# Gate and up products with the activations stationary, two PSUM banks in turn, and a short warm-up

## The chip, the core and the metric

The kernel runs on one core of a Trainium2 chip. The metric is the device time of one execution in microseconds (us). Everything is float32 in and out; matrix products are made from a high part and a low part of each operand (below).

## The reference

Two layers of a transformer on 256 tokens of width 2048. Each layer is: half a SwiGLU feed-forward block (FFN), a mixer, half an FFN. Layer 0 has a gated delta-rule and pooling mixer (GDN), layer 1 a latent attention mixer (MLA). Only the FFN and the output projections of the mixers matter here.

```python
def swiglu(h, w_gate, w_up, w_down):
    return (jax.nn.silu(h @ w_gate) * (h @ w_up)) @ w_down

for layer in range(DEPTH):                    # DEPTH = 2
    x = x + 0.5 * swiglu(rms_norm(x, ffn1_norm[layer]), ...)   # gate, up: 2048 x 4096, down: 4096 x 2048
    h = rms_norm(x, mix_norm[layer])
    x = x + delta_pool_mixer(h, ...)  if layer % 2 == 0 else  x + mla_mixer(h, ...)
    x = x + 0.5 * swiglu(rms_norm(x, ffn2_norm[layer]), ...)
```

So there are four FFNs.

## The kernel before

**Split products.** Each float32 operand is split into a high part (a cast to the rounded type fp32r) and a low part (the rest). A product is high times high, plus low weight times high activation, plus high weight times low activation. Weights come from memory in tiles `raw` of 128 x 2048 (1 MB, three buffers, SyncE's queue). `piece` (L167, L168) makes of each half of such a tile a `whi` on ScalarE (ACT) and a `wlo` on VectorE (DVE), 128 x 1024, four buffers each. The normalized activations lie in 16 tiles `xg[k]` of 128 features x (high 256 tokens, low 256 tokens), made by `feed_part` (L155, L156).

**Gate and up, before.** The hidden width of 4096 goes in 32 blocks f of 128. For each f, `gemm` runs over the 16 k and `mm3` issues two products: the stationary operand is a 128 x 128 block of `whi`, and the moving operand is the whole of `xg[k]`, 512 columns (high and low tokens side by side in one PSUM bank); then a block of `wlo` is stationary and the high half, 256 columns, is moving. All products of one f go to one bank. The result is features x tokens, the layout that the down product needs. `scaled` adds the two halves (L436, L437), multiplies by the norm factor `R` (L438; `end_norm` spreads it over the partitions by a product on TensorE, L371), then come Silu (L131), gate times up (L459) and the split into the tiles `g` (L152, L153).

**Down and mixer outputs.** In `project` the activations are stationary (128 x 128: one half t of the tokens) and the weights move, 512 columns at a time. For each of 4 column blocks j and each k (32 for an FFN, 16 for a mixer) six products go out: three in a row to the bank of t = 0, three to the bank of t = 1. Then L398 adds the result to x.

**Order of work.** The program is written out by hand and a scheduler orders each engine's queue by it, with a model of the times. `Chains` holds generators (`spawn`, `poll`) whose steps are woken by a clock that the issued products move; `yield n * LAG` asks for a distance of n x 1500 ns of such clock. `feed_norm` uses this: four transposes on TensorE (L361) are put into a running product at such a distance after the values they need.

**Start.** `constants` calls `warm_up`: zeros are multiplied while the first loads are under way. Eight products of plain float32 (L281) are followed by rows of products of several forms (L288), among them one row of eight fp32r products of 512 columns into one bank and one row of eight in which two banks take turns, all with start and stop set. The first FFN then begins with `opening`, which loads the activations in four parts and the first two blocks f of gate and up.

PSUM has eight banks of 128 x 512 float32; in an FFN six serve products (`mm`) in rotation and two the transposes (`aux`).

Of the kernel before, what the change touches and what calls it, by code (L numbers as in the profile page):

```python
# [18 lines left out]
P = 128  # L19
S = 256  # L20
D = 2048
KT = 16
DFF = 4096
NF = 32
# [15 lines left out]
LAG = 1500.0  # L40
# [3 lines left out]
SILU = "silu_and_others"  # L44
# [53 lines left out]
class Builder:  # L98
# [89 lines left out]
    def gemm(self, ps, stream, acts, wide=True):  # L188

        K = len(acts)  # L190
        for k0 in range(0, K, 8):
            self.gemm_piece(ps, next(stream), acts, k0, wide)
# [76 lines left out]

    def warm_up(self):  # L270

        nc = self.nc
        z = self.tmp([P, S], "res")
        nc.vector.memset(z, 0.0)
        zr = self.wp.tile([P, 2048], F32R, tag="raw", bufs=3, name=self.nm("zr"))
        nc.vector.memset(zr.bitcast(F32), 0.0)
        zb = z.bitcast(BF16)
        self.banks(7, 1)
        ps = self.psum("aux")
        for n in range(8):  # L280
            nc.tensor.matmul(ps[:, 0:S], z[:, 0:P], z, start=n == 0, stop=n == 7)  # L281
        a, b = self.psum("mm"), self.psum("mm")
        w = zr[:, 1024:1152]

        def row(rhs, count, outs=(a,), lhsT=w):
            size = int(np.prod(rhs.shape[1:]))
            for n in range(count):
                nc.tensor.matmul(outs[n % len(outs)][:, 0:size], lhsT, rhs, start=True, stop=True)  # L288

        row(zr[:, 0:512], 8)  # L290
        row(zr[:, 0:512], 8, (a, b))
        row(zb, 6, lhsT=zb[:, 0:P])
        row(zr[:, 0:256], 8)
        row(zr[:, 0:384], 6)
        row(zr.rearrange("p (a c) -> p a c", a=2)[:, :, 0:256], 6)
        row(zr[:, 0:1024].rearrange("p (c a) -> p c a", a=2)[:, :, 0], 6)
        row(zr[:, 4:516], 6)
        row(zr[:, 16:528], 6)
        row(zr[:, None, 0:256].to_broadcast([P, 2, 256]), 6)
        row(z, 4, lhsT=z[:, 0:P])  # L300

    def load_xf(self, c):

# [64 lines left out]
    def end_norm(self, after):  # L368
# [3 lines left out]
        self.behind(m, after)  # L372
        R = self.tp.tile([P, S], F32, tag="R", bufs=1, name=self.nm("R"))
        self.nc.scalar.copy(R, ps[:, :S])
        return R

    def project(self, slabs, acts, half, after):

        K = len(acts)
        st = self.weights(*[slabs[j] for j in range(4)])  # L380
        blk = [slice(0, P), slice(P, 2 * P)]
        for j in range(4):
            ps = [self.psum("mm") for _ in range(2)]
            for k in range(K):
                if k % 2 == 0:
                    piece = next(st)
                hi, lo = (w[:, 512 * (k % 2) : 512 * (k % 2) + 512] for w in piece)
                self.ch.wait(lambda: acts[k] is not None)
                a = acts[k]
                for t in range(2):  # L390
                    self.mm(ps[t], a[:, 0, blk[t]], hi, start=k == 0, stop=False)
                    self.mm(ps[t], a[:, 0, blk[t]], lo, start=False, stop=False)
                    self.last_mm = self.mm(ps[t], a[:, 1, blk[t]], hi, start=False, stop=k == K - 1)
                self.ch.poll()
            for t in range(2):
                x = self.x[j][:, t, :]
                if half:
                    self.nc.vector.scalar_tensor_tensor(x, ps[t], 0.5, x, op0=ALU.mult, op1=ALU.add)  # L398
                else:
                    self.nc.vector.tensor_tensor(x, ps[t], x, op=ALU.add)  # L400
            after(j)


    def ffn(self, wg, wu, wd, after, start=False):
        nc, tc = self.nc, self.tc
        with tc.tile_pool(name=self.nm("gp"), bufs=1) as gp:
            self.banks(6, 2)
            xg = self.xg

            def opening():  # L410

                ps = [self.psum("mm") for _ in range(4)]
                for c in range(4):
                    raw = self.raw_tile()
                    k4 = slice(512 * c, 512 * c + 512)
                    self.load_xf(c)
                    for w, src in enumerate((wg, wu)):
                        dst = raw[:, 1024 * w : 1024 * w + 1024].rearrange("p (f k) -> p f k", f=2)
                        nc.sync.dma_start(dst, src[0:2, :, k4].rearrange("f p k -> p f k"))
                    for w in range(2):  # L420
                        hi, lo = self.piece(raw, 1024 * w)
                        for n in range(8):
                            k = 4 * c + n % 4
                            n128 = slice(n * P, n * P + P)
                            self.last_mm = self.mm3(ps[2 * (n // 4) + w], hi[:, n128], lo[:, n128], xg[k], k == 0, k == KT - 1, True)
                self.load_rest()
                return ps

            def ws():
                for f in range(2 if start else 0, NF):  # L430
                    yield from self.weights(wg[f], wu[f])

            def scaled(ps):

                t, u = (gp.tile([P, S], F32, tag=n, bufs=3, name=self.nm(n)) for n in ("t", "u"))
                nc.scalar.copy(u, ps[:, S : 2 * S])  # L436
                nc.vector.tensor_tensor(t, ps[:, 0:S], u, op=ALU.add)  # L437
                nc.vector.tensor_tensor(t, t, R, op=ALU.mult)  # L438
                return t

            st = ws()
            g = []
            early = opening() if start else []
            for f in range(NF):
                if early:
                    pg, pu = early.pop(0), early.pop(0)
                else:
                    pg, pu = self.psum("mm"), self.psum("mm")
                    self.gemm(pg, st, xg)
                    if f == 0:  # L450
                        self.gemm(pu, st, xg)
                if f == 0:
                    R = self.end_norm(self.last_mm)
                tg = scaled(pg)
                self.table(SILU, tg, tg, AF.Silu)
                if f > (1 if start else 0):
                    self.gemm(pu, st, xg)
                tu = scaled(pu)
                nc.vector.tensor_tensor(tu, tu, tg, op=ALU.mult)  # L459
                gt = gp.tile([P, 2, S], F32R, name=self.nm("g"))  # L460
                self.split_hi_lo(gt, tu)
                g.append(gt)
            self.project(wd, g, True, after)

    def store(self, j):
        for t in range(2):
# [3 lines left out]
def gdn(b, after):  # L470
# [7 lines left out]
    with tc.tile_pool(name="gd", bufs=1) as gp:  # L478
# [18 lines left out]
        for t in range(2):  # L497
# [321 lines left out]
def mla(b, after):  # L819
# [8 lines left out]
    with tc.tile_pool(name="ml", bufs=1) as gp:  # L828
# [183 lines left out]
        for p in range(MH // 2):  # L1012
# [57 lines left out]
def slabs(w):  # L1070

    K, N = w.shape
    return w.reshape(K // P, P, N // P, P).transpose(2, 1, 0, 3).reshape(N // P, P, K)


def wide_slabs(w):

    K = w.shape[0]
    return w.reshape(K // P, P, 4, 512).transpose(2, 1, 0, 3).reshape(4, P, 4 * K)


def columns(v, n):

    return v.reshape(n, P).T
# [20 lines left out]
def prepare(a):  # L1105
    n = {}
# [4 lines left out]
    g = [columns(a[k][l], KT) for l in range(2) for k in ("ffn1_norm", "mix_norm", "ffn2_norm")]  # L1111
    n["gains"] = np.stack(g, 1)
    for f in ("1", "2"):
        for s, k in (("g", "gate"), ("u", "up"), ("d", "down")):
            lay = wide_slabs if s == "d" else slabs
            n[f"w{f}{s}"] = np.stack([lay(a[f"ffn{f}_w_{k}"][l]) for l in range(2)])
    w = a["hyb_w_in"][0]
    u = slabs(np.concatenate([w[:, :4096], w[:, 4112:]], 1))
    n["wqk"] = np.stack([u[8 * c + h] for h in range(GH) for c in range(2)])
# [12 lines left out]
    w = a["hyb_w_out"][0]  # L1132
    n["wgo"] = wide_slabs(np.concatenate([w[:1024]] + [w[1024 + P * c : 1152 + P * c] for c in POOL_ORDER], 0))
    w = a["mla_w_in"][0]
# [38 lines left out]
```

## Time and profile before

| | |
|---|---|
| median of 2 runs | 2904.0 us (2903.99 to 2904.01) |
| profiled execution | 2904.99 us, of which the span of the trace is 2903.2 us |
| TensorE, products | busy 2895.9 us (100%), 16272 products |
| VectorE / ScalarE / GpSimd | busy 1776.9 us (61%) / 1462.9 us (50%) / 57.5 us (2%) |
| memory | 509.84 MB read, 176 GB/s over the span |

In the rows PE is TensorE (PEld its weight loads), DVE VectorE, ACT ScalarE. A product's duration in the rows includes a modelled tail that overlaps the next product; the distance from one start to the next is what TensorE's time is made of.

### The profile page before, as it was taken

Reading aid. Unit: us, or ns where it says so; the run is one execution under the profiler, and the core shown is the slowest. Engines: PE = TensorE matmul, PEld = TensorE weight load, DVE = VectorE, ACT = ScalarE, POOL = GpSimd, SP = SyncE. Lnnn points to the kernel's source line nnn. Section 1 sums busy time; section 2 is a strip of 40 time slices with the busy share of each in tenths; the row PEclk is TensorE's granted clock in tenths of the full one; section 3 lists DMA queues with packets and bytes.
Section 4 is the critical chain, followed back from the end, with each engine's and each line's share of the span. In section 5 each row is a group of like instructions: output and inputs, shape, how many; then the busy total and the mean of one; then the engine's idle time right before and its main releaser. Section 6 shows DMA issues by size and latency. Waiting matters only on the chain.

```text
span 2903.2 us, 39987 instructions
## 1 busy us (share of the span) xinstructions
PE 2895.9 (100%) x16272; PEld 2492.8 (86%) x16272; DVE 1776.9 (61%) x2532; ACT 1462.9 (50%) x2222; POOL 57.5 (2%) x97
## 2 busy tenths in 40 slices
PE   9999999999999999999999999999999999999999
PEld 8888888899998888888888888888898788888887
DVE  5666655576785666665546666645677566666544
ACT  5444444466374544444445444544577554444433
POOL 0000000000000000000000000000022000000000
PEclk9999999999999999999999999999999999999999
DMA  6555555544235555555555555555533445555554
GB/s 235 189 187 181 185 189 187 181 149 173 102 142 181 181 185 186 188 189 189 182 183 187 187 182 185 186 189 188 179 135 113 145 174 189 189 182 186 187 202 143
DMA packets 77256, 514.65 MB, mean 177 GB/s; under 512 B 10768, under 2 KB 11536, under 8 KB 16272
## 3 DMA queue, kind: packets, MB, share of 16 engines
q1 hardware_dynamic: 75344, 508.90, 49.4%
q8 instruction: 127, 2.08, 0.3%
q0 software_dynamic: 576, 2.10, 0.2%
q10 hardware_dynamic: 1152, 1.10, 0.1%
q14 instruction: 57, 0.47, 0.1%
HBM read 509.84 MB, written 2.10 MB: 176 GB/s over the span
## 4 chain that ended last, share of the span: by engine, by line
PE 98%; issue 1%; ACT 0%; DVE 0%; POOL 0%; DMA 0%; ACTq 0%; POOLq 0%; DVEq 0%
PE mm L186 92%; PE aux L186 4%; PE mm L288 1%; PE aux L361 1%; PE aux L281 0%; PE aux L681 0%; PE aux L997 0%; ACT sq L336 0%; POOL osq L221 0%; DMA cb<-in_wab 0%; PE aux L371 0%; ACT L126 0%; ACT whi L167 0%; ACT xg L155 0%; DVE x L398 0%
## 5 line engine op out<-in xcount | busy, mean ns | idle before, releaser
L186 PE MATMUL mm<-xg,whi 128*128 128x512 f32 (+1 forms) x5664 | 1720.6, 368 | 0.6 <-ACT xg L155 0.3
L168 DVE TENSOR_TENSOR wlo<-raw,whi 128x1024 fp32r<-128x1024 f32 x960 | 1175.2, 1225 | 747.1 <-ACT whi L167 737.5
L167 ACT CAST whi<-raw 128x1024 fp32r<-128x1024 f32 x960 | 1007.0, 1049 | 761.3 <-PE mm L186 736.5
L186 PE MATMUL mm<-xg,wlo 128*128 128x256 f32 x4880 | 1329.6, 281 | 0.0
L186 PEld LDWEIGHTS mm<-xg,whi 128*128 128x128 f32 x5664 | 997.7, 189 | 168.6 <-DVE xg L156 1.5
L186 PEld LDWEIGHTS mm<-xg,wlo 128*128 128x128 f32 x4880 | 923.2, 189 | 25.7
L186 PE MATMUL mm<-whi,g 128*128 128x512 f32 x2048 | 648.5, 396 | 0.0
L186 PEld LDWEIGHTS mm<-whi,g 128*128 128x128 f32 x2048 | 384.0, 187 | 92.9
L186 PE MATMUL mm<-wlo,g 128*128 128x512 f32 x1024 | 404.5, 395 | 0.0
L436 ACT COPY u<-mm 128x256 f32<-128x256 f32 x256 | 95.1, 372 | 463.4 <-PE mm L186 463.4
L437 DVE TENSOR_TENSOR t<-mm,u 128x256 f32<-128x256 f32 x256 | 108.6, 425 | 246.8 <-ACT u L436 246.7
L186 PEld LDWEIGHTS mm<-wlo,g 128*128 128x128 f32 x1024 | 192.0, 188 | 46.0
L438 DVE TENSOR_TENSOR t<-t,R 128x256 f32<-128x256 f32 x256 | 108.5, 425 | 8.4
L186 PE MATMUL mm<-whi,o 128*128 128x512 f32 x256 | 84.2, 399 | 0.0
L152 ACT CAST g<-t 128x256 fp32r<-128x256 f32 x128 | 52.1, 407 | 56.9 <-DVE t L459 56.9
L221 POOL TENSOR_TENSOR sq<-sqf,sq 128x256 fp32r<-128x256 f32 x49 | 45.4, 932 | 1337.2 <-ACT sq L220 1324.1
L186 PEld LDWEIGHTS mm<-whi,o 128*128 128x128 f32 x256 | 47.9, 187 | 11.1 <-DVE o L153 0.2
L459 DVE TENSOR_TENSOR t<-t,t 128x256 f32<-128x256 f32 x128 | 54.5, 426 | 4.8 <-ACT t L131 0.2
L155 ACT ACTIVATE xg<-aux,gains 128x256 fp32r<-128x256 f32 x80 | 37.1, 471 | 38.9 <-DVE xg L156 27.5
L131 ACT ACTIVATE t<-t 128x256 f32<-128x256 f32 x128 | 53.5, 418 | 5.8 <-DVE t L438 5.4
L153 DVE TENSOR_TENSOR g<-t,g 128x256 fp32r<-128x256 f32 x128 | 53.5, 418 | 0.0
L186 PE MATMUL mm<-wlo,o 128*128 128x512 f32 x128 | 50.5, 395 | 0.0
(267 smaller groups left out, 1560.6 us busy)
## 6 DMA issues: line engine op xcount, KB each, us to landing
raw<-in_w1d SPq DMA_DIRECT2D x64, 1024.0 KB, 4.8
raw<-in_w2g SPq DMA_DIRECT2D x64, 1024.0 KB, 4.8
raw<-in_w2u SPq DMA_DIRECT2D x64, 1024.0 KB, 4.8
raw<-in_w2d SPq DMA_DIRECT2D x64, 1024.0 KB, 4.8
raw<-in_w1g SPq DMA_DIRECT2D x62, 1024.0 KB, 4.8
raw<-in_w1u SPq DMA_DIRECT2D x62, 1024.0 KB, 4.8
raw<-in_wqk SPq DMA_DIRECT2D x16, 1024.0 KB, 4.8
raw<-in_wgo SPq DMA_DIRECT2D x16, 1024.0 KB, 4.8
```

The costliest lines, as they stand in the source:

```text
L131: a = nc.scalar.activation(out, in_, func, **kw)
L152: nc.scalar.copy(dst[:, 0, :], src)
L153: nc.vector.tensor_tensor(dst[:, 1, :], src, dst[:, 0, :].bitcast(F32), op=ALU.subtract)
L155: nc.scalar.activation(dst[:, 0, :], src, AF.Copy, scale=scale)
L167: self.nc.scalar.copy(hi, raw[:, h : h + 1024])
L168: self.nc.vector.tensor_tensor(lo, raw[:, h : h + 1024], hi.bitcast(F32), op=ALU.subtract)
L186: return self.nc.tensor.matmul(out, lhsT, rhs, start=start, stop=stop)
L221: nc.gpsimd.tensor_tensor(dst[:, 1, :], sq, dst[:, 0, :].bitcast(F32), op=ALU.subtract)
L436: nc.scalar.copy(u, ps[:, S : 2 * S])
L437: nc.vector.tensor_tensor(t, ps[:, 0:S], u, op=ALU.add)
L438: nc.vector.tensor_tensor(t, t, R, op=ALU.mult)
L459: nc.vector.tensor_tensor(tu, tu, tg, op=ALU.mult)
```

## The change

Gate and up are computed as the down product is: `columns` takes 512 hidden columns at a time (8 blocks instead of 32), the activations are stationary, the weights move. `rows` issues the six products of a k with the two banks (token halves t) in turn: high-high t0, t1; low weights t0, t1; low activations t0, t1. `project` uses the same functions, so the down products and both mixers' output projections take turns too. The result is now tokens x features: `gated` applies Silu with the norm factor `r2` as a scale per partition, `hidden` multiplies gate and up, transposes the 128 x 128 blocks back on TensorE (eight per block of 512) and splits them into `g`. `end_norm` is no longer called by the FFN. `opening` loads whole 1 MB tiles of the first 512 columns of gate and up. The weights of gate and up are laid out on the host as those of down are. The warm-up keeps its eight plain float32 products alone.

```diff
     def warm_up(self):
-        z = self.tmp([P, S], "res")
-        zr = self.wp.tile([P, 2048], F32R, tag="raw", bufs=3, name=self.nm("zr"))
...
+        z = self.tmp([P, S], "res", 1)
+        self.nc.vector.memset(z, 0.0)
         self.banks(7, 1)
         ps = self.psum("aux")
         for n in range(8):
+            self.nc.tensor.matmul(ps[:, 0:S], z[:, 0:P], z, start=n == 0, stop=n == 7)
-        row(zr[:, 0:512], 8)
-        row(zr[:, 0:512], 8, (a, b))
...
+    def rows(self, ps, hi, lo, act, first, last):
+        blk = [slice(0, P), slice(P, 2 * P)]
+        for part, w in ((0, hi), (0, lo), (1, hi)):
+            end = last and part == 1
+            for t in range(2):
+                self.last_mm = self.mm(ps[t], act[:, part, blk[t]], w, start=first and w is hi and part == 0, stop=end)
+
+    def columns(self, stream, acts):
+        K = len(acts)
+        ps = [self.psum("mm") for _ in range(2)]
+        for k in range(K):
+            if k % 2 == 0:
+                piece = next(stream)
+            hi, lo = (w[:, 512 * (k % 2) : 512 * (k % 2) + 512] for w in piece)
+            self.ch.wait(lambda: acts[k] is not None)
+            self.rows(ps, hi, lo, acts[k], k == 0, k == K - 1)
+            self.ch.poll()
+        return ps
+
     def project(self, slabs, acts, half, after):
         for j in range(4):
-                for t in range(2):
-                    self.mm(ps[t], a[:, 0, blk[t]], hi, start=k == 0, stop=False)
-                    self.mm(ps[t], a[:, 0, blk[t]], lo, start=False, stop=False)
-                    self.last_mm = self.mm(ps[t], a[:, 1, blk[t]], hi, start=False, stop=k == K - 1)
+            ps = self.columns(st, acts)
...
             def opening():
+                ps = [[self.psum("mm") for _ in range(2)] for _ in range(2)]
                 for c in range(4):
                     self.load_xf(c)
+                    raws = [self.raw_tile() for _ in range(2)]
+                    for raw, src in zip(raws, (wg, wu)):
+                        nc.sync.dma_start(raw, src[0][:, 2048 * c : 2048 * c + 2048])
+                    for h in range(2):
+                        for w in range(2):
+                            hi, lo = self.piece(raws[w], 1024 * h)
+                            for n in range(2):
+                                k = 4 * c + 2 * h + n
+                                c512 = slice(512 * n, 512 * n + 512)
+                                self.rows(ps[w], hi[:, c512], lo[:, c512], xg[k], k == 0, k == KT - 1)
...
+            def gated(ps):
+                sg = gp.tile([P, 2, 512], F32, tag="sg", bufs=2, name=self.nm("sg"))
+                for t in range(2):
+                    self.table(SILU, sg[:, t, :], ps[t], AF.Silu, scale=self.r2[:, t : t + 1])
+                return sg
+
+            def hidden(f, ps, sg):
+                for t in range(2):
+                    nc.vector.scalar_tensor_tensor(sg[:, t, :], ps[t], self.r2[:, t : t + 1], sg[:, t, :], op0=ALU.mult, op1=ALU.mult)
+                yield 1.5 * LAG
+                for h in range(2):
+                    pt = self.psum("aux")
+                    for n in range(2):
+                        for t in range(2):
+                            c = (2 * h + n) * P
+                            nc.tensor.transpose(pt[:, (2 * n + t) * P : (2 * n + t + 1) * P], sg[:, t, c : c + P], self.ident)
+                            self.ch.clock += P / 2.4
+                    gt = gp.tile([P, 2, 2, S], F32R, name=self.nm("g"))
+                    flat = lambda part: gt[:, part].rearrange("p n s -> p (n s)")
+                    nc.scalar.copy(flat(0), pt)
+                    nc.vector.tensor_tensor(flat(1), pt, flat(0).bitcast(F32), op=ALU.subtract)
+                    for n in range(2):
+                        g[4 * f + 2 * h + n] = gt[:, :, n, :]
+                    yield 0.5 * LAG
...
-            for f in range(NF):
+            for f in range(NC):
+                if f == 0 and start:
+                    pg, pu = opening()
+                    sg = gated(pg)
                 else:
+                    pg = self.columns(st, xg)
+                    sg = gated(pg)
+                    pu = self.columns(st, xg)
+                self.ch.spawn(hidden(f, pu, sg))
+                self.ch.poll()
+            self.project(wd, LateList(lambda k: g[k], NF), True, after)
```

## Rows read from the trace of the kernel before

**Rows 1.** The page: busy time by engine, and the granted clock in 40 slices.

```profile
PE 2895.9 (100%) x16272; PEld 2492.8 (86%) x16272; DVE 1776.9 (61%) x2532; ACT 1462.9 (50%) x2222; POOL 57.5 (2%) x97
...
PEclk9999999999999999999999999999999999999999
```

**Rows 2.** The page: the chain that ended last, by line.

```profile
PE mm L186 92%; PE aux L186 4%; PE mm L288 1%; PE aux L361 1%; PE aux L281 0%; PE aux L681 0%; PE aux L997 0%; ACT sq L336 0%; POOL osq L221 0%; DMA cb<-in_wab 0%; PE aux L371 0%; ACT L126 0%; ACT whi L167 0%; ACT xg L155 0%; DVE x L398 0%
```

**Rows 3.** Timeline of TensorE, last FFN: start us, duration us, instruction.

```profile
2369.14 0.59 PE L371 MATMUL aux<-dg,ca 128*128 128x256 f32 x2
2369.39 0.58 PE L186 MATMUL mm<-xg,whi 128*128 128x512 f32 x1
...
2719.97 0.39 PE L186 MATMUL mm<-whi,g 128*128 128x512 f32 x1
...
2898.23 0.63 PE L186 MATMUL mm<-whi,g 128*128 128x512 f32 x2
2898.69 0.40 PE L186 MATMUL mm<-wlo,g 128*128 128x512 f32 x1
2898.93 0.39 PE L186 MATMUL mm<-whi,g 128*128 128x512 f32 x1
```

**Rows 4.** Groups by form, 2370 to 2719 us: count, busy us, mean ns of one.

```profile
L186 PE MATMUL mm<-xg,whi 128*128 128x512 f32 x989 | 344.6, 399 | 0.0
L186 PE MATMUL mm<-xg,wlo 128*128 128x256 f32 x989 | 267.9, 281 | 0.0
```

**Rows 5.** Groups by form, 2721 to 2898 us.

```profile
L186 PE MATMUL mm<-whi,g 128*128 128x512 f32 x507 | 159.5, 395 | 0.0
...
L398 DVE SCALAR_TENSOR_TENSOR x<-mm,x 128x512 f32<-128x512 f32 x6 | 3.8, 683 | 0.0
```

**Rows 6.** Groups by form, 8.2 to 9.5 us: warm-up, one bank.

```profile
L288 PE MATMUL mm<-zr 128*128 128x512 f32 x7 | 1.8, 394 | 0.0
```

**Rows 7.** Groups by form, 9.95 to 11.2 us: warm-up, two banks in turn.

```profile
L288 PE MATMUL mm<-zr 128*128 128x512 f32 x7 | 1.7, 389 | 0.0
```

**Rows 8.** Groups by form, 20.25 to 21.35 us: warm-up, one bank, another offset.

```profile
L288 PE MATMUL mm<-zr 128*128 128x512 f32 x7 | 1.8, 392 | 0.0
```

**Rows 9.** Groups by form, 54.1 to 58.3 us: gate and up, first FFN.

```profile
L186 PE MATMUL mm<-xg,whi 128*128 128x512 f32 x12 | 4.2, 391 | 0.0
L186 PE MATMUL mm<-xg,wlo 128*128 128x256 f32 x14 | 3.8, 280 | 0.0
```

**Rows 10.** Timeline of TensorE around four transposes of feed_norm.

```profile
435.19 0.39 PE L186 MATMUL mm<-whi,g 128*128 128x512 f32 x1
435.41 0.60 PE L361 MATMUL aux<-ca,x 128*128 128x128 f32 x4
435.77 0.48 PE L186 MATMUL mm<-whi,g 128*128 128x512 f32 x1
436.09 0.39 PE L186 MATMUL mm<-wlo,g 128*128 128x512 f32 x1
```

**Rows 11.** Timeline of TensorE at the start.

```profile
1.22 6.63 PE L281 MATMUL aux<-res 128*128 128x256 f32 x16 [1.22 <-DVE res L274]
7.50 4.03 PE L288 MATMUL mm<-zr 128*128 128x512 f32 x16
...
24.45 0.91 PE L186 MATMUL mm<-xg,whi 128*128 128x512 f32 x2
```

**Rows 12.** Timeline of ACT at the start.

```profile
6.49 1.03 ACT L167 CAST whi<-raw 128x1024 fp32r<-128x1024 f32 x1
8.83 1.05 ACT L167 CAST whi<-raw 128x1024 fp32r<-128x1024 f32 x1 [1.31 <-DMA raw<-in_w1u]
...
11.78 1.03 ACT L167 CAST whi<-raw 128x1024 fp32r<-128x1024 f32 x1
```

**Rows 13.** Groups by form, 1 to 6 us: the first warm-up products.

```profile
L281 PE MATMUL aux<-res 128*128 128x256 f32 x11 | 5.1, 649 | 1.2 <-DVE res L274 1.2
```

**Rows 14.** Groups by form, 23 to 24 us: the last warm-up products.

```profile
L288 PE MATMUL mm<-res 128*128 128x256 f32 x6 | 1.5, 379 | 0.0
```

**Rows 15.** The page: splitting the weights on DVE.

```profile
L168 DVE TENSOR_TENSOR wlo<-raw,whi 128x1024 fp32r<-128x1024 f32 x960 | 1175.2, 1225 | 747.1 <-ACT whi L167 737.5
```

More of the change, by code (lines that the diff above doesn't have):

```diff
@@ L270, in warm_up @@
     def warm_up(self):
-        nc = self.nc
-        z = self.tmp([P, S], "res")
-        nc.vector.memset(z, 0.0)
-        zr = self.wp.tile([P, 2048], F32R, tag="raw", bufs=3, name=self.nm("zr"))
-        nc.vector.memset(zr.bitcast(F32), 0.0)
-        zb = z.bitcast(BF16)
+        z = self.tmp([P, S], "res", 1)
+        self.nc.vector.memset(z, 0.0)
         self.banks(7, 1)
@@ L280, in warm_up @@
         for n in range(8):
[L281 to L288, printed above, removed]
-        row(zr[:, 0:512], 8)
-        row(zr[:, 0:512], 8, (a, b))
[L292 to L300, printed above, removed]
+            self.nc.tensor.matmul(ps[:, 0:S], z[:, 0:P], z, start=n == 0, stop=n == 7)
     def load_xf(self, c):
@@ L375, in end_norm @@
         return R
+    def rows(self, ps, hi, lo, act, first, last):
[15 more added lines that the diff above has]
+        return ps
     def project(self, slabs, acts, half, after):
-        K = len(acts)
         st = self.weights(*[slabs[j] for j in range(4)])
-        blk = [slice(0, P), slice(P, 2 * P)]
         for j in range(4):
[L383 to L389, printed above, removed]
-                for t in range(2):
-                    self.mm(ps[t], a[:, 0, blk[t]], hi, start=k == 0, stop=False)
-                    self.mm(ps[t], a[:, 0, blk[t]], lo, start=False, stop=False)
-                    self.last_mm = self.mm(ps[t], a[:, 1, blk[t]], hi, start=False, stop=k == K - 1)
-                self.ch.poll()
+            ps = self.columns(st, acts)
             for t in range(2):
@@ L405, in ffn @@
         nc, tc = self.nc, self.tc
+        NC = DFF // 512
         with tc.tile_pool(name=self.nm("gp"), bufs=1) as gp:
@@ L408, in ffn @@
             xg = self.xg
+            g = [None] * NF
             def opening():
-                ps = [self.psum("mm") for _ in range(4)]
+                ps = [[self.psum("mm") for _ in range(2)] for _ in range(2)]
                 for c in range(4):
-                    raw = self.raw_tile()
-                    k4 = slice(512 * c, 512 * c + 512)
                     self.load_xf(c)
[L417 to L425, printed above, removed]
+                    raws = [self.raw_tile() for _ in range(2)]
[8 more added lines that the diff above has]
+                                self.rows(ps[w], hi[:, c512], lo[:, c512], xg[k], k == 0, k == KT - 1)
                 self.load_rest()
@@ L429, in ws @@
             def ws():
-                for f in range(2 if start else 0, NF):
+                for f in range(1 if start else 0, NC):
                     yield from self.weights(wg[f], wu[f])
[L433 to L439, printed above, removed]
@@ L441, in ffn @@
-            st = ws()
-            g = []
-            early = opening() if start else []
-            for f in range(NF):
-                if early:
-                    pg, pu = early.pop(0), early.pop(0)
-                else:
[L448 to L462, printed above, removed]
@@ L463, in ffn @@
-            self.project(wd, g, True, after)
+            def gated(ps):
[21 more added lines that the diff above has]
+                    yield 0.5 * LAG
@@ L1076, in wide_slabs @@
 def wide_slabs(w):
-    K = w.shape[0]
-    return w.reshape(K // P, P, 4, 512).transpose(2, 1, 0, 3).reshape(4, P, 4 * K)
+    K, N = w.shape
+    return w.reshape(K // P, P, N // 512, 512).transpose(2, 1, 0, 3).reshape(N // 512, P, 4 * K)
 def columns(v, n):
@@ L1114, in prepare @@
         for s, k in (("g", "gate"), ("u", "up"), ("d", "down")):
-            lay = wide_slabs if s == "d" else slabs
-            n[f"w{f}{s}"] = np.stack([lay(a[f"ffn{f}_w_{k}"][l]) for l in range(2)])
+            n[f"w{f}{s}"] = np.stack([wide_slabs(a[f"ffn{f}_w_{k}"][l]) for l in range(2)])
     w = a["hyb_w_in"][0]
```

## The prediction

> **What bounds the kernel now.** I read the page's busy times first: TensorE is busy for the whole span, VectorE for 61% and ScalarE for 50%, and the granted clock stands at full speed in every slice [rows 1]. The chain that ended last says the same from the other side: 92% of it is the line that issues all products [rows 2]. So only what changes TensorE's own time can count: the number of products, the distance from the start of one to the start of the next, and stretches in which it does something useless (the warm-up). Work taken from VectorE and ScalarE is worth nothing here, and it stays hidden as long as TensorE is not made to wait.
>
> The columns that gate and up stream do not change: 768 per k and block of 128 before (512 + 256), six times 512 per k and block of 512 after, which is again 768 per 128. What changes is how they are cut into products, so the distance between starts is the number to find. The timeline of the last FFN gives it. From 2369.39 to 2719.97 us there are 31 blocks x 2 x 16 = 992 pairs, 353.4 ns a pair [rows 3, 4]. From there to the last product at 2898.93 there are 767 steps of the down product, 233.3 ns each [rows 3]. A mean duration of 395 ns in the groups thus goes with a distance of 233 [rows 5]: the tail of 162 ns overlaps the next product, and I use that difference to turn other durations into distances.
>
> **The change part by part.**
>
> *Gate and up.* 4 FFNs x 32 x 2 x 16 = 4096 pairs cost 4096 x 0.3534 = 1447.5 us. They become 4 x 8 x 2 x 16 x 6 = 6144 products of 512 columns of the form that the down product has. At its 233.3 ns they cost 1433.4 us: 14.1 us less, from the cut alone.
>
> *Taking turns.* Does it shorten the distance? The warm-up holds the nearest rows. Seven products into one bank average 394 ns, the seven after them, with two banks in turn and nothing else changed, 389 [rows 6, 7]; a later row into one bank has 392 [rows 8]. The gain is 3 to 5 ns a product. These are products of zeros with one stationary block and without accumulation, so I also look for the effect in the body, where `project` changes bank after every third product. Across the change two products take 2898.69 - 2898.23 = 0.46 us, and the next, without a change, 2898.93 - 2898.69 = 0.24 [rows 3]: no gain at a single change. And the same one-bank pairs that average 399 and 281 ns in the last FFN average 391 and 280 for some microseconds of the first [rows 4, 9], so the distance can settle at several values with no change of bank at all. The bounds are therefore 0 and the full step down to the alternating row's own distance, 389 - 162 = 227 ns; I take the middle of the warm-up's gain, 4 ns, since only that row alternates at every product. The distance is then 229.3 ns: gate and up 6144 x 0.2293 = 1408.8 us, 38.7 less than before, and the down and output products, 4 x 4 x 32 x 6 + 2 x 4 x 16 x 6 = 3840, gain 3840 x 0.004 = 15.4 us.
>
> *Transposes.* Eight per block of 512, 4 x 8 x 8 = 256, in 64 groups of four, all on TensorE's path. Around such a group of `feed_norm` two products and four transposes take 436.09 - 435.19 = 0.90 us; less two products of 0.233 that is 0.433 us a group [rows 10]. 64 x 0.433 = 27.7 us are added. The groups carry 0.60 us for four, which is mostly tail. The Trainium skill (TensorE: Matmul & The Clock Gate, Part 4: PE-mode transpose) gives about 275 ns for a transpose in a kernel's context; as an estimate from that page 256 of them would cost 70 us and leave no gain. The row decides against it here: 0.11 us from start to start.
>
> *Waits that come with them.* The transposes need gate times up, which VectorE forms out of PSUM: two operations like L398's, 683 ns each [rows 5], behind at most one weight split of 1225 ns in flight [rows 15], 2.6 us after the last up product. `hidden` yields 1.5 x 1500 ns of product clock in between; that clock counts 213 ns for a product that really takes 229, so about 2.4 us of real products are queued ahead. The wait is 0 to 0.2 us a block, 0 to 6 us in all; I take 0, because TensorE's timeline shows none before the transposes that `feed_norm` places in the same way [rows 10]. Behind a late transpose the whole product stream is queued. The rest of the tail, ScalarE's copy and VectorE's subtraction, has 28 more steps of k before `project` reads the last `g`. ScalarE's Silu now waits for gate's last product with weight splits behind it, as its copy of the same result did before; four `whi` buffers, some 11 us of products, cover 1.3 us of Silu. SyncE's loads keep their size of 1 MB and their rate.
>
> *`end_norm`.* Two instructions and the product behind them start 0.25 us apart and stretch it from 0.40 to 0.58: 0.43 us [rows 3], four times, 1.7 us less.
>
> *Warm-up.* The first real product now starts at 24.45 us, because the rows of products run till then [rows 11]. The weights were there long before: the first 0.5 MB tile's half was being split at 6.49 us, the second at 8.83 [rows 12]. Now the first tile is 1 MB, so it lands when both of these had, about 8.8; its split takes 1.05 us, and the first product can start at 9.9. That is 14.5 us earlier. The up tile follows 1 MB later; by the next split's start, 11.78 after 8.83 [rows 12], it is ready at 12.8 against 12.65 when gate's first twelve products are through, 0.2 us of waiting. After that each quarter keeps TensorE for 11 us and loads 2.5 MB, at the start's pace 7 us: no further wait. There is a hole from 7.9 to 9.9 us, after the eight products that remain. The first products ran at the lower clock level (649 ns against 379 for the same form later, 1.2 against 2.4 GHz) from 1.22 us nearly to the start of the first row at 7.50 [rows 11, 13, 14], which cost about 2.8 us. If the hole brings that back it costs as much again; I take half, 1.3. The start saves 13.0 us, between 11 and 14.5.
>
> **Sum.** -38.7 - 15.4 + 27.7 - 1.7 - 13.0 = -41.1 us on the profiled execution, whose 2904.99 us lie 1.0 above the median of the runs. From the median 2904.0: 2863 us, 1.4% faster. Own range of this case, with 3 and 5 ns and the bounds of start and waits: 2848 to 2877.
>
> **The rivals.**
>
> 1. Taking turns pays nothing: the steps of `project` say so, the alternating warm-up row against it. Then -14.1 + 27.7 - 1.7 - 13.0 = -1.1, 2903 us, and the cut, the start and the transposes just cancel.
>
> 2. Taking turns pays in full, the body running at the alternating row's own 227.3 ns: gate and up 1396.5, 51.0 less; 3840 x 0.006 = 23.0 less; 13.0 more for the three other terms: -61.0, 2843 us. For it, the distance in [rows 9], 391 - 162 = 229 ns, shows that the body can run near that value.
>
> 3. Slower: the transposes stand too early in TensorE's queue. If nothing were queued between the last up product and them, each of the 32 blocks would stop TensorE for the 2.6 us above, 83 us on top of the forecast: 2946 us. It decides where the lead falls to 1.3 us: the other 1.3 us a block then eat all of the 41. Against it stands that `feed_norm`'s transposes start with no gap.
>
> 4. Slower: the clock. The bank change could let TensorE starve between products and drop its clock. In this trace the clock reads full speed while banks alternate in the warm-up and while `project` changes them [rows 1]. If each of the 88 sums of products that begin on a fresh pair of banks paid the start's 2.8 us, that would be 246 us more, 3109. The Trainium skill (the same page, "A second HAM failure mode: psum-queue depth-cycling") tells of such an oscillation where banks are cycled at 512 columns; the trace does not agree with it here.
>
> **How the numbers follow.** The forecast gets 0.46, rival 1 0.26, rival 2 0.20, rivals 3 and 4 together 0.06; 0.02 is left for a distance above 235 ns, which costs 30 us or more. The predicted time is the forecast's. The range reaches from half of rival 2 to just past rival 1 with its waits, 2838 to 2908; what lies outside is the slow cases and the lower half of rival 2. About 2%, 58 us, is what a measurement of this kernel tells from no change: under 2846 lies most of rival 2, so faster 0.18, slower 0.06, and the same 0.76.
>
> **What the changed profile would show.** Products of gate and up with 512 columns only, with a mean near 391 ns (395 would be rival 1, 389 rival 2), and the down products moved by the same amount. 256 more transposes on the path, 0.43 us for each four, with no wait on VectorE before them. The first real product near 10 us. TensorE still busy for all of the span. The prediction is wrong if the distance between products depends on what moves and what is stationary rather than on banks, or if a wait shows before the transposes.

## The result and the profile after

The changed kernel takes 2871.82 us (median of 2 runs) against 2904.0 before: a ratio of 0.9889, 95% interval 0.9847 to 0.9932, 32 us less. The forecast was 2863 with a range of 2838 to 2908. The profiled execution took 2871.58 us, its span 2869.5 us, 33.7 less than the span before.

The page after, busy times, granted clock and chain, to be held against [rows 1, 2]:

```profile
PE 2855.3 (100%) x14398; PEld 2402.4 (84%) x14398; DVE 1556.6 (54%) x1891; ACT 1360.1 (47%) x1834; POOL 57.5 (2%) x97
...
PEclk9999999999999999999999999999999999999999
...
PE mm L186 91%; PE aux L186 4%; PE aux L435 1%; PE aux L338 1%; DMA x<-in_x 0%; PE aux L674 0%; PE aux L990 0%; DMA xf<-in_xf 0%; POOL osq L221 0%; DMA cb<-in_wab 0%; ACT sq L313 0%; ACT whi L167 0%; DVE xg L156 0%; PE aux L714 0%; ACT xg L155 0%
```

TensorE still bounds the kernel alone; the new transposes (L435) stand on the chain, and a load of x, which stood nowhere before, appears in it.

The timeline of TensorE after, at the boundaries of the last FFN (as [rows 3]):

```profile
2329.04 0.40 PE L186 MATMUL mm<-whi,xg 128*128 128x512 f32 x1
...
2684.80 0.63 PE L186 MATMUL mm<-whi,g 128*128 128x512 f32 x2
...
2864.39 0.62 PE L186 MATMUL mm<-whi,g 128*128 128x512 f32 x2
```

Gate and up take 2684.80 - 2329.04 = 355.76 us for 1536 products and 16 groups of four transposes. Such a group after (timeline, as [rows 10]):

```profile
107.10 0.62 PE L186 MATMUL mm<-whi,xg 128*128 128x512 f32 x2
107.56 0.60 PE L435 MATMUL aux<-ca,sg 128*128 128x128 f32 x4
107.91 0.71 PE L186 MATMUL mm<-whi,xg 128*128 128x512 f32 x2
108.46 0.62 PE L186 MATMUL mm<-wlo,xg 128*128 128x512 f32 x2
```

Four products and four transposes take 108.46 - 107.10 = 1.36 us; less 4 x 0.227 that is 0.45 us a group, with no gap in front. So a product of gate and up takes (355.76 - 16 x 0.45) / 1536 = 226.9 ns from start to start. The down product, issued by the same lines, has its last product 0.23 us behind the last row's 2864.39, at 2864.62, 179.8 us after its first: (179.8 - 2 x 0.45) / 767 = 233.3, as before. The groups by form show the same step, 389 to 391 against 395 ns (first 2330 to 2684 us, as [rows 4], then 2686 to 2864 us, as [rows 5]):

```profile
L186 PE MATMUL mm<-whi,xg 128*128 128x512 f32 x1020 | 277.3, 391 | 0.0
...
L186 PE MATMUL mm<-wlo,xg 128*128 128x512 f32 x510 | 157.5, 389 | 0.0
```

```profile
L186 PE MATMUL mm<-whi,g 128*128 128x512 f32 x508 | 139.6, 395 | 0.0
```

That is the riddle of this case: the same function, the same weight buffers, the same turns between banks, and two distances.

The start after, TensorE's timeline (as [rows 11]), ScalarE's (as [rows 12]), and busy time and granted clock in two stretches:

```profile
1.22 5.18 PE L277 MATMUL aux<-res 128*128 128x256 f32 x16 [1.22 <-DVE res L273]
8.95 0.74 PE L186 MATMUL mm<-whi,xg 128*128 128x512 f32 x2 [2.54 <-ACT whi L167]
10.21 0.73 PE L186 MATMUL mm<-wlo,xg 128*128 128x512 f32 x2 [0.52 <-DVE wlo L168]
10.78 1.67 PE L186 MATMUL mm<-whi,xg 128*128 128x512 f32 x4
12.25 1.05 PE L186 MATMUL mm<-wlo,xg 128*128 128x512 f32 x2
13.11 1.05 PE L186 MATMUL mm<-whi,xg 128*128 128x512 f32 x2
17.68 2.17 PE L186 MATMUL mm<-whi,xg 128*128 128x512 f32 x4 [3.52 <-ACT whi L167]
...
20.50 1.46 PE L186 MATMUL mm<-whi,xg 128*128 128x512 f32 x4
```

```profile
7.86 1.04 ACT L167 CAST whi<-raw 128x1024 fp32r<-128x1024 f32 x1 [0.87 <-DMA raw<-in_w1g]
15.97 0.63 ACT L313 ACTIVATE sq<-x 128x512 f32<-128x512 f32 x1 [7.08 <-DMA x<-in_x]
...
16.60 2.92 ACT L167 CAST whi<-raw 128x1024 fp32r<-128x1024 f32 x3
```

```profile
10.00:15.00 5.00, 3.95 (x10) 2.61 (x10) 0.16 (x1) 0.00 (x0) 0.00 (x0) 0.66 1.02 416
15.00:20.00 5.00, 2.32 (x5) 1.52 (x6) 2.34 (x3) 4.03 (x7) 0.00 (x0) 0.79 0.14 54
```

The first real product starts at 8.95 us, a little earlier than forecast, but after twelve products TensorE stands still for 3.52 us: ScalarE's next instruction is a square of x (L313), which waits 7.08 us for its load, and the next three weight splits are queued behind it. The granted clock (third column from the right) reads 0.66 and 0.79 in the two stretches, 1.2 GHz for part of each. The products from 11.4 us on take twice their time, so the clock fell before this hole, and those behind the hole run at the low level as well. Full speed is back at about 21.3 us with 20 products done, worth a start at 21.3 - 20 x 0.227 = 16.8 us at full speed. The start saved 24.45 - 16.8 = 7.6 us, not 13.

### The profile page after: what moved, and what is told of

The parts are those of the page before. It is cut to its first block, busy times and chain, and to the rows that moved or that the text cites. A ratio compares the mean times of both kernels' runs of the same rounds, so it can differ in the third digit from the quotient of the medians.

```text
span 2869.5 us, 35434 instructions
## 1 busy us (share of the span) xinstructions
PE 2855.3 (100%) x14398; PEld 2402.4 (84%) x14398; DVE 1556.6 (54%) x1891; ACT 1360.1 (47%) x1834; POOL 57.5 (2%) x97
## 4 chain that ended last, share of the span: by engine, by line
PE 98%; issue 1%; DMA 1%; ACT 0%; DVE 0%; POOL 0%; DVEq 0%; ACTq 0%; SPq 0%; POOLq 0%
PE mm L186 91%; PE aux L186 4%; PE aux L435 1%; PE aux L338 1%; DMA x<-in_x 0%; PE aux L674 0%; PE aux L990 0%; DMA xf<-in_xf 0%; POOL osq L221 0%; DMA cb<-in_wab 0%; ACT sq L313 0%; ACT whi L167 0%; DVE xg L156 0%; PE aux L714 0%; ACT xg L155 0%
## 5 line engine op out<-in xcount | busy, mean ns | idle before, releaser
L186 PE MATMUL mm<-whi,xg 128*128 128x512 f32 x4096 | 1115.2, 391 | 6.1 <-ACT whi L167 6.1
L186 PEld LDWEIGHTS mm<-whi,xg 128*128 128x128 f32 x4096 | 765.4, 188 | 163.7 <-ACT whi L167 7.8
L186 PE MATMUL mm<-wlo,xg 128*128 128x512 f32 x2048 | 632.7, 390 | 0.5 <-DVE wlo L168 0.5
L186 PE MATMUL mm<-whi,g 128*128 128x512 f32 x2048 | 567.6, 396 | 0.0
L186 PEld LDWEIGHTS mm<-wlo,xg 128*128 128x128 f32 x2048 | 385.0, 188 | 81.6 <-DVE wlo L168 1.0
L186 PE MATMUL mm<-wlo,g 128*128 128x512 f32 x1024 | 321.8, 395 | 0.0
L186 PE MATMUL mm<-xg,whi 128*128 128x256 f32 x1568 | 291.2, 286 | 0.3 <-ACT xg L155 0.3
L186 PEld LDWEIGHTS mm<-xg,whi 128*128 128x128 f32 x1568 | 245.2, 192 | 1.7 <-ACT xg L155 0.5
L186 PE MATMUL mm<-xg,wlo 128*128 128x256 f32 x784 | 221.7, 283 | 0.0
L186 PEld LDWEIGHTS mm<-xg,wlo 128*128 128x128 f32 x784 | 150.0, 191 | 0.0
```

Source lines behind the costliest of these rows:

```text
L186: return self.nc.tensor.matmul(out, lhsT, rhs, start=start, stop=stop)
```

## The experiments

Each is the changed kernel with the edit shown, unless it says otherwise. Means below are of 512-column products in the groups by form, last FFN unless a stretch is named; 389 to 391 ns go with 227 ns from start to start, 394 to 399 with 232 to 237.

### Three in a row instead of turns

```diff
-        for part, w in ((0, hi), (0, lo), (1, hi)):
-            for t in range(2):
+        for t in range(2):
+            for part, w in ((0, hi), (0, lo), (1, hi)):
```

> The changed kernel with one thing undone: the six products of a k go three in a row to the bank of t = 0 and then three to the bank of t = 1, as in the down product of the kernel before; everything else is as changed. In the changed kernel gate and up run at 227 ns from start to start and the down products, issued by the same function, at 233. Theory A, taking turns is what brought gate and up to 227: without it they go back to about 233 ns, 6144 x 0.0065 = 40 us more, near 2912 us, and down stays at 233. Rival, the cut alone (activations stationary, 512 columns of weights moving) did it: gate and up stay at 227 and the time at 2872 us.

Measured 2871.84 us, ratio 0.9887 (0.9873 to 0.9902). Groups by form, gate and up, then down:

```profile
L186 PE MATMUL mm<-whi,xg 128*128 128x512 f32 x995 | 310.5, 391 | 0.0
```

```profile
L186 PE MATMUL mm<-whi,g 128*128 128x512 f32 x486 | 152.9, 395 | 0.0
```

Without turns gate and up run exactly as fast. Theory A, and with it the forecast's term for turns, falls.

### Twelve in a row

```diff
-        for k in range(K):
...
+        for k0 in range(0, K, 4):
+            pieces = [next(stream), next(stream)]
+            for t in range(2):
+                for k in range(k0, k0 + 4):
...
+                    self.rows(ps, hi, lo, acts[k], k == 0, k == K - 1, (t,))
```

`rows` runs over the given t alone, so a bank is kept for twelve products and then the other one for twelve.

> The changed kernel with twenty-four products in a row: for two pieces of weights (four k) the twelve products of t = 0 and then the twelve of t = 1, instead of turns. Three in a row to one bank ran gate and up at 227 ns just as turns did. Theory: banks have no part in the distance, and gate and up stay at 227, down at 233; the time is near 2872, or some microseconds more where two pieces at a time leave less room for the next ones. Rival: three in a row is still often enough, and long stays in one bank bring 231 ns or more, as the warm-up's row into one bank had: gate and up then cost 6144 x 0.004 = 25 us more.

One run: 2870.63 us. Gate and up:

```profile
L186 PE MATMUL mm<-whi,xg 128*128 128x512 f32 x1009 | 314.8, 391 | 0.0
```

Twelve products in one bank change nothing either. Banks have no part in the 227.

### The down product with the other stationary operand

```diff
+            own = after == self.store
-            self.project(wd, LateList(lambda k: g[k], NF), True, after)
+            self.project(wd, LateList(lambda k: None if g[k] is None else xg[k % KT] if own else g[k], NF), True, after)
```

> The changed kernel, but the down product of the last FFN takes the activation tiles of gate and up (xg[k mod 16]) as its stationary operand instead of g; this changes what is computed. The other three FFNs are left as they are. Theory P, the distance goes with the stationary operand (where its tile lies, or what it holds): the last down product runs at 227 ns while the first three stay at 233, and the time falls by 768 x 0.0065 = 5 us. Rival S, it goes with the stage (its weights, its banks, the length of its sums): the last down product stays at 233 and the time at 2872.

The last down product leaves out g, so this run does not compute the layer; it is there for its times. One run: span 2864.1 us, 5.4 less than the changed kernel's. Groups by form, 2690 to 2850 us, the last down product:

```profile
L186 PE MATMUL mm<-whi,xg 128*128 128x512 f32 x472 | 126.3, 389 | 0.0
```

The step went to 227 ns in the down stage, with its weights, banks and sums; the first three stayed at 395 to 396. It goes with the stationary operand.

### The weights below the activations

```diff
-        self.xp = pool("xp", 1)
         self.wp = pool("wp", 4)
+        self.xp = pool("xp", 1)
```

> The changed kernel with the weight buffers placed in SBUF below the activations xg instead of above them (two pools in the other order); the tiles g stay above both. In the changed kernel xg, which runs at 227 ns, lies below the weights, and g and the mixers' outputs, which run at 233, lie above. Theory P1, the place of the stationary tile beside that of the moving one decides: gate and up now go to 233 ns like down, 40 us more, near 2912. Rival, place does not matter: 227 and 233 as before, 2872.

Measured 2872.0 us, and gate and up (391 ns) and down (395) kept their distances. Which of the two lies higher does not matter. But the swap moved the tiles by whole multiples of 2048 bytes, and so left something as it was: their offsets within small powers of two.

### The tiles g shifted by some bytes

The placement of the tiles in the compiled program says that the weights and xg start 32 bytes past a multiple of 256, g at one.

```diff
             self.banks(6, 2)
             xg = self.xg
+            self.pads = getattr(self, "pads", [8, 16, 32, 456])
+            pad = gp.tile([P, self.pads.pop(0)], F32, name=self.nm("pad"))
+            nc.gpsimd.memset(pad, 0.0)
```

> The changed kernel with a pad in front of the tiles sg and g, of 32, 64, 128 and 1824 bytes in the first to fourth FFN. Without pads g starts on a multiple of 64 bytes and the weights and xg lie 32 bytes past one; with 32 and 1824 bytes g has the offset of the weights and of xg, with 64 and 128 it has not. Theory A, the offset of the stationary operand modulo 64 bytes (alone, or beside that of the moving operand) decides between 227 and 233 ns: the down products of the first and fourth FFN run at 227, of the second and third at 233, and the time falls by 2 x 768 x 0.0064 = 10 us, to 2862. Rival D, what the tile holds (how g is made, its values) decides: all four stay at 233 and 2872 us.

Measured 2863.05 us, ratio 0.9857 (0.9837 to 0.9876). The four down products in order (four stretches, one line each):

```profile
L186 PE MATMUL mm<-whi,g 128*128 128x512 f32 x490 | 133.0, 391 | 0.0
...
L186 PE MATMUL mm<-whi,g 128*128 128x512 f32 x491 | 136.6, 397 | 0.0
...
L186 PE MATMUL mm<-whi,g 128*128 128x512 f32 x496 | 138.3, 398 | 0.0
...
L186 PE MATMUL mm<-whi,g 128*128 128x512 f32 x485 | 130.0, 389 | 0.0
```

With pads of 32 and 1824 bytes the down product is fast, with 64 and 128 slow, 8.8 us in all for two of four (10 were expected). What the tile holds is out: g holds the same values in all four cases that it held before.

### Everything shifted by 32 bytes

```diff
         self.eps = self.cst.tile([P, 1], F32, name="eps")
+        pad = self.cst.tile([P, 8], F32, name="pad")
+        nc.gpsimd.memset(pad, 0.0)
```

> The changed kernel with one pad of 32 bytes in the first pool, so that everything behind it moves by 32: xg and the weights to a multiple of 64, g and the mixers' outputs to 32 past one. Theory A1, the stationary operand's own offset decides (32 past a multiple of 64 is the fast one): gate and up go to 233 ns, 40 us more, and down to 227, 20 us less, together near 2892. Theory A2, the offsets of stationary and moving operand have to be equal modulo 64: gate and up stay at 227, down at 233, 2872. Theory A3, the moving operand's offset decides nothing and the rival D of the other run holds: the same as A2, and then the shifted g of the other run stays at 233.

Measured 2871.98 us. Gate and up, then down:

```profile
L186 PE MATMUL mm<-whi,xg 128*128 128x512 f32 x1008 | 274.2, 391 | 0.0
```

```profile
L186 PE MATMUL mm<-whi,g 128*128 128x512 f32 x487 | 133.5, 395 | 0.0
```

Nothing changed. So it is not the stationary operand's own offset (A1); with the run before, it is the difference between the two operands' offsets (A2).

### Which modulus

The edit is the one of the shifted g with pads of 24, 40, 72 and 8 floats.

> The changed kernel with pads of 96, 160, 288 and 32 bytes in front of sg and g in the four FFNs; the offsets of g and the weights then differ by 64, 128, 256 and 0 bytes, modulo 512 with the fourth's 256 as well. A difference of 32 or 96 and of 64 from the other side was slow. Theory M128: only the difference modulo 128 bytes counts: the first FFN's down product at 233 ns, the other three at 227. Theory M256: the first two at 233, the other two at 227. Rival: no rule of this kind, the fourth alone at 227.

One run: 2863.18 us. The four down products in order:

```profile
L186 PE MATMUL mm<-whi,g 128*128 128x512 f32 x492 | 136.7, 397 | 0.0
...
L186 PE MATMUL mm<-whi,g 128*128 128x512 f32 x492 | 136.7, 396 | 0.0
...
L186 PE MATMUL mm<-whi,g 128*128 128x512 f32 x492 | 133.3, 390 | 0.0
...
L186 PE MATMUL mm<-whi,g 128*128 128x512 f32 x485 | 130.0, 389 | 0.0
```

A difference of 64 bytes is slow, of 128 slow, of 256 fast: M256. All cases together, stationary minus moving operand modulo 256 bytes (placement of the compiled programs):

| difference | where | mean ns (`whi`) |
|---|---|---|
| 0 | xg after; everything shifted: xg; pads 32, 1824, 288: g | 389 to 391 |
| 32, 64, 96, 128 | pads 64; 96; 128; 160: g | 396 to 398 |
| 64, 96 | mixers' outputs, after | 396 to 400 |
| 224 | g after; everything shifted: g | 395 |

The mixers' 399 and 400 are no third distance: those means hold the products beside transposes.

### The squares behind the splits

```diff
-        self.nc.scalar.copy(hi, raw[:, h : h + 1024])
+        self.cast = self.nc.scalar.copy(hi, raw[:, h : h + 1024])
...
+            if cast is not None:
+                self.behind(a, cast)
```

`opening` notes the cast of each quarter and `load_rest` passes that of the third to the squares and to the cast of the ones.

> The changed kernel with the squares of x (and the cast of the ones) queued on ScalarE behind the weight split of the third quarter of the opening. In the changed kernel ScalarE stood 7.08 us in front of the first square, which waited for x, with the next weight splits behind it, and TensorE waited 3.5 us for them and then ran at the lower clock for some microseconds. Theory: the order on ScalarE is what cost the start; the hole of TensorE near 13.5 us falls under 1 us, the clock is back at full speed by about 15 us instead of 21, and the time falls by 4 to 6 us, to about 2867. Rival, the up tile itself lands late because all loads share the queues: the splits wait for it instead and the time stays within 1 us of 2872.

Measured 2864.94 us, ratio 0.9866 (0.9849 to 0.9882): 6.9 us less than the changed kernel, a little more than the 4 to 6 expected. ScalarE's timeline and the windows:

```profile
10.33 2.96 ACT L167 CAST whi<-raw 128x1024 fp32r<-128x1024 f32 x3 [1.47 <-DMA raw<-in_w1u]
```

```profile
10.00:15.00 5.00, 4.83 (x21) 3.98 (x22) 3.71 (x5) 4.56 (x7) 0.00 (x0) 1.00 1.02 424
15.00:20.00 5.00, 5.00 (x24) 4.14 (x23) 4.21 (x9) 2.76 (x5) 1.03 (x2) 1.00 0.96 358
```

The up tile had landed at 10.3 us; only the order on ScalarE kept its splits until 16.6. Without that hole the clock reads 1.00 through both stretches. Not all of the low clock belongs to the hole, though: in the changed kernel it fell at about 11 us, before it. That first fall cost nothing. In the run with three in a row these twelve products ran at full speed, and the thirteenth still started at 17.73 us, against 17.68.

### The short warm-up alone

The kernel before, with `warm_up` of the changed one.

> The kernel before with the short warm-up alone. Theory: the rows of products only held up the first real product, whose weights lie ready at 7 to 10 us, but the opening's four quarters land until about 21 us and ScalarE's squares stand between the splits, so TensorE waits for data: the time falls by 8 to 14 us, to about 2893. Rival: the clock drops in the holes and the splits behind ScalarE's squares take back most of it, less than 6 us gained.

Measured 2898.35 us, ratio 0.9976 (0.9966 to 0.9986): 6.5 us less, between the two expectations; the nine runs lie between 2895.72 and 2899.65. In ScalarE's waits of the first 50 us, in TensorE's timeline and in the windows stand the reasons:

```profile
ACT sq L313 <- DMA x<-in_x: 7.8, 4, 4.1
```

```profile
37.81 1.22 PE L348 MATMUL aux<-dg,ca 128*128 128x256 f32 x2 [2.76 <-DVE dg L324]
```

```profile
30.00:40.00 10.00, 5.54 (x22) 4.26 (x23) 6.01 (x15) 8.97 (x20) 0.00 (x0) 0.85 0.35 119
40.00:50.00 10.00, 10.00 (x49) 8.65 (x48) 8.19 (x15) 5.50 (x11) 0.00 (x0) 0.81 0.57 211
```

The squares hold up the splits here as well (7.8 us of waiting), and the norm factor that follows from them comes 2.8 us late for `end_norm`. Around that wait the granted clock falls to 0.85 and 0.81, as the rival had it. The long warm-up had hidden this order: in the kernel before TensorE waits for nothing from 24 to 60 us.

### The offset in the kernel before

```diff
         self.ps = pool("ps", 1, space=PSUM)
+        self.nc.gpsimd.memset(self.tp.tile([P, 8], F32, tag="pad", bufs=1, name="pad"), 0.0)
```

This is the kernel before with one pad of 32 bytes ahead of all that an FFN or a mixer allocates.

> The kernel before with one edit: a pad of 32 bytes ahead of everything that an FFN or a mixer allocates, so that the tiles g have the offset of the weights modulo 128. Theory: the down products go from 233 to 227 ns with three products in a row to a bank, 3072 x 0.0064 = 20 us less (25 with the delta-rule mixer's outputs): 2881 to 2885, and gate and up stay at 353 ns a pair. Rival: in the kernel before something else holds the down product at 233, and the time stays at 2904.

Measured 2884.75 us, ratio 0.9932 (0.9915 to 0.9949), 19.3 less. Down, 2706 to 2876 us, then gate and up:

```profile
L187 PE MATMUL mm<-whi,g 128*128 128x512 f32 x501 | 154.2, 389 | 0.0
```

```profile
L187 PE MATMUL mm<-xg,whi 128*128 128x512 f32 x850 | 296.3, 399 | 0.0
```

One pad in the old kernel brings more than half of what the change brought. The old gate and up products stay at 399 and 281 ns although their operands' offsets are equal (weights and xg, both at 32): with the weights stationary and the activations moving, equal offsets do not bring the short distance.

### Both remedies, and all offsets equal

The version with the squares behind, with the pad of the run before ahead of the pools, and 32 bytes more in the latent mixer:

```diff
         self.ps = pool("ps", 1, space=PSUM)
+        self.nc.gpsimd.memset(self.tp.tile([P, 8], F32, tag="pad", bufs=1, name="pad"), 0.0)
...
+        nc.gpsimd.memset(tl([P, 8], "pad"), 0.0)
```

> The changed kernel with three small edits: the squares queued behind the third quarter's weight split; a pad of 32 bytes ahead of everything that an FFN or a mixer allocates, which puts g at the offset of the weights (32 past a multiple of 256); a further 32 bytes in the latent mixer, so that its outputs o, and those of the delta-rule mixer, lie 128 bytes from the weights' offset modulo 256. Theory: start 6.9 us less, the four down products at 227 ns, 3072 x 0.0064 = 20 us less: 2845. If only the offset modulo 128 counts, the mixers' output products (768) go to 227 as well, 5 us less: 2840. Rival: the two do not add, because a faster down product waits for its weights or for x: above 2855.

Measured 2846.41 us, ratio 0.9801 (0.9786 to 0.9816): the two add. Groups by form, down, then the latent mixer's output product, whose offset was still 128 off:

```profile
L187 PE MATMUL mm<-whi,g 128*128 128x512 f32 x427 | 114.2, 389 | 0.0
```

```profile
L187 PE MATMUL mm<-whi,o 128*128 128x512 f32 x252 | 72.4, 399 | 0.0
L187 PE MATMUL mm<-wlo,o 128*128 128x512 f32 x126 | 39.6, 394 | 0.0
```

Then with 128 bytes more of pad in both mixers, the delta-rule mixer first:

```diff
+        nc.gpsimd.memset(tl([P, 32], "pad"), 0.0)
...
-        nc.gpsimd.memset(tl([P, 8], "pad"), 0.0)
+        nc.gpsimd.memset(tl([P, 40], "pad"), 0.0)
```

> The run with squares behind and pads, with 128 bytes more of pad in both mixers, so that their outputs too lie at the weights' offset modulo 256; before that they lay 128 bytes off and ran at 232 to 234 ns. Theory M256 (stationary and moving operand at the same offset modulo 256 bytes): the 768 output products of the mixers go to 227 ns as well, 768 x 0.0064 = 5 us less: 2841. Rival: the rule holds for xg and g alone and the mixers' outputs are held by something else: they stay near 233 and the time at 2846.

Measured 2842.69 us, ratio 0.9789 (0.9776 to 0.9803). The same output product:

```profile
L187 PE MATMUL mm<-whi,o 128*128 128x512 f32 x249 | 70.4, 395 | 0.0
L187 PE MATMUL mm<-wlo,o 128*128 128x512 f32 x124 | 38.4, 390 | 0.0
```

The rule holds for these operands too: both rows fall by 4 ns, and the time by 3.7 us where 5 were expected. (The mean of `whi` stays at 395 because it holds the products beside transposes.) This version beats both kernels: 61 us under the kernel before, 29 under the changed one.

## Why the prediction was right, and where it was not

The time lay in the range and the direction was right, but two terms that held the sum were wrong, in opposite directions, and the start was put too high.

| term | forecast us | measured us | from |
|---|---|---|---|
| gate and up: cut and turns | -38.7 | -53.4 | 1447.5 - 6144 x 0.2269 |
| down and output products | -15.4 | 0 | 233.3 ns before and after; the latent mixer's outputs have 399 and 395 ns in both |
| transposes | +27.7 | +28.8 | 64 x 0.45 |
| `end_norm` | -1.7 | -1.7 | not measured apart |
| start | -13.0 | -7.6 | 24.45 - 16.8 |
| sum | -41.1 | -33.9 | spans: -33.7 |

*Taking turns* is the step that failed. It read 4 ns out of the warm-up's alternating row [rows 6 to 8] and spread it over all products. The run with three in a row shows that turns give 0 ns. The evidence against was in the same step: no gain at `project`'s single changes [rows 3], and two distances with one bank in the body [rows 4, 9]. That gate and up and down together came out within 1 us of the forecast (-53.4 against -54.1) is a coincidence: gate and up got rival 2's distance in full, the other products rival 1's.

*Gate and up, the cut.* The step priced the new products by the down product's row, 233.3 ns, because the form is the same. That row was 6.4 ns too slow for them: g lies off the weights' offset modulo 256, xg does not. The prediction had named this, a distance that depends on what moves and what is stationary, as what would make it wrong. Shown by moving g (down goes to 227 by 32 bytes) and by putting xg in its place. So of the 53.4 us 14.1 are the cut as the step priced it, and the other 39.3, 6144 x 0.0064, are the shorter distance; turns are no part of it. No run moved xg alone off the weights' offset, so that gate and up would then run at 233 is inferred from g.

*Start.* The first product came even earlier than the step said, at 8.95 us against 9.9; what failed is its "no further wait". The step checked loads and products and not what else stands in ScalarE's queue. The squares of x, an instruction that was harmless as long as the warm-up filled TensorE, had become the wait that ends last. The term measured 7.6 us instead of 13; the missing 5.4 are nearly all of the error of the sum (7.2; the other two are the transposes, 1.1, and 0.7 of the products). The run with the squares behind gives 6.9 back. The clock, which the step feared for the first hole, did fall at about 11 us, but it cost its time only behind the second hole.

*Transposes and their waits* held: 0.45 us a group against 0.433, and no gap before them. The Trainium skill's 275 ns for a transpose (TensorE: Matmul & The Clock Gate, Part 4: PE-mode transpose) is near the duration of a row here, 272 ns. As a price it is not borne out, as four transposes add 0.45 us. Rival 3 did not show. Rival 4 did not either in the body, where the clock reads full speed while banks take turns; only at the start did it fall.

Two of the prediction's sums are slightly off: with its own bounds the case's range is 2852 to 2881 us, not 2848 to 2877, and half of 2.8 us is 1.4.

**Open.** Why a difference of offsets costs 6.4 ns is not shown, only that it does. Two rows with equal offsets stay unexplained: the old gate and up pairs at 353.4 ns, which the two distances alone (226.9 and, for 256 columns, 281 - 162 = 119 by the prediction's way from durations to distances) would put near 346 (most of the excess is in the 512 columns, 399 - 162 = 237), and the warm-up's row into one bank at 394 ns, whose operands lie 4096 bytes apart in one tile.

## What to carry to other kernels

Before a product is priced by a row of the same form, compare where the operands of both lie: here 32 bytes decided 3% of every down product, and one pad of 32 bytes brought 19 us in the kernel before. When a cover of useless work is taken away, read the whole in-order queue of every engine that feeds the bottleneck in that stretch, not only the loads and the products. A probe row that differs from the body in several ways (start and stop set, one stationary block) is no price for one of them; undo that one thing in the kernel itself.

## What the hardware showed unexpectedly

- With the activations stationary and the weights moving, fp32r products of 128 x 128 by 512 columns start 226.9 ns apart when the byte offsets of the two operands in SBUF are equal modulo 256, and 233 to 234 ns apart in the cases with a difference of 32, 64, 96, 128 or 224 bytes. With the roles exchanged, in the kernel before, equal offsets left the 512 columns at 399 ns a row.
- One bank for 12 products in a row, 3 in a row or turns after every product make no difference to that, 391 ns each.
- In the runs with the hole of 3 to 5 us in front of the thirteenth product the products behind it soon ran at the low clock level (0.79 from 15 to 20 us in the changed kernel); in the three without it, the one with the squares behind and the two built on it, the clock stayed at 1.00.
- The length of the first hole, in front of the first real product, did not decide whether the clock fell already between the two: it did with 2.5 us (the changed kernel, at about 11 us) and with 1.1 us (twelve in a row, everything shifted), and did not with 1.4 to 2.4 us in seven others. What decided it stays open.
